# Modulation products of a two-block network: whole 1 MB pieces through the weights' ring instead of quarter pieces with a ring of their own

## The chip, the cores and the metric

The kernel runs on one core of a Trainium2 chip, alone. Every time is in microseconds (us) on the device. The kernel was timed in three runs: 2586.94, 2588.70 and 2591.15 us, median 2588.7. One further execution was recorded by the profiler; all rows below come from that one.

The engines are named as the profile names them: PE multiplies matrices (PEld is its loading of the stationary operand), DVE and ACT do elementwise work, POOL is a third, slower elementwise engine, and SP issues nearly all the transfers from DRAM. Each engine runs its instructions in the order in which they were written out at build time; SP does too, so that a transfer whose buffer is not free holds up all transfers behind it.

## The reference

A first block (norm, a mixer with recurrences and attention, output product, feed-forward) is followed by two layers of a second block. Each of these layers is steered by modulation vectors, which depend on nothing but the two vectors `c` and `c_ctx`:

```python
def ada_mods(cvec, w, b):                      # w [1024, 6144], b [6144]
    m = jax.nn.silu(cvec) @ w + b
    return jnp.split(m[:, None, :], 6, axis=-1)

def modulate(h, shift, scale):
    return h * (1.0 + scale) + shift

def first_block(x, ...):                       # one layer
    z = rms_norm(x, norm_mix[l]) @ w_in[l]
    ...                                        # four mixers of 256 columns each
    x = x + mixed @ w_out[l]
    gu = rms_norm(x, norm_ffn[l]) @ w_gate_up[l]
    return x + (silu(gu[..., :D_FF]) * gu[..., D_FF:]) @ w_down[l]

def second_block(x, c, ctx, c_ctx, ada_w, ada_b, ...):
    for l in range(2):
        sh1_l, sc1_l, ga1_l, sh2_l, sc2_l, ga2_l = ada_mods(c, ada_w[l], ada_b[l])
        sh1_c, sc1_c, ga1_c, sh2_c, sc2_c, ga2_c = ada_mods(c_ctx[None, :], ada_w[l], ada_b[l])
        hl = modulate(rmsnorm(xl, norm1_g[l]), sh1_l, sc1_l)
        ...                                    # mixer, expert feed-forward
```

Here `x` has 512 tokens of 1024 features and `ctx` 256 tokens. Everything is float32. The modulation products of a layer multiply 2 rows by a matrix of 24 MB, so that both layers read 48 MB for them.

## The kernel before

Products of activations and weights are done in three passes with a high and a low part of each operand. `wload` (line 190) brings a weight block of up to [128, 2048] float32 (1 MB) into a buffer of the tag `raw`, a ring of three (two in the projection of layer 0), and `split` makes `hi` on ACT (line 208) and `lo` on DVE (line 209) from it, each in a ring of two. The raw buffer is free once both have read it.

The modulation products run beside other work. `ada_setup` lists 192 pieces (layer, group g of 2048 columns, block k of 128 rows, quarter j of 512 columns). `fill(n)` (line 874) emits the next n of them at the place of the call. `ada_piece` (line 876) loads 128 x 512 float32 (256 KB) into a ring of its own, of four buffers in the first block and three in layer 0 (`ada_open`), and multiplies it with one matrix product (line 883): the stationary operand has 32 columns (two are used), and quarter j goes to column group j of the array (`tile_position=(0, 32 * j)`), so that four quarters fill the 128 rows of one PSUM bank. After eight k the bank gets its bias (line 892), is written to DRAM as rows (line 894) and turned into columns (line 898).

`fill` is called with 8 before each of the four token tiles of the attention's preparation in the first block (line 558), with 2 after each of its 32 attention units (line 686), with 5 before each projection of layer 0 (line 979), and at the end with what is left (line 936). The first 96 pieces belong to layer 0, the others to layer 1.

The order in which instructions stand on an engine is not that of the source: a scheduler writes it out at build time. It moves instructions past others where data and buffers allow.

The stages of the profile around the change are, by time in the recorded execution: preparation of the attention (141.5 to 204.6 us, with a tile of relative-position biases written to DRAM as `skewd` and read back as `skew`), the attention (to 345.5), the output product with `w_out` (`b1_out`, lines 758 to 789, to 410), the norm before the feed-forward (`norm_T`, line 230, to about 436) and the feed-forward (to 797), the norm of layer 0 (to 823), and the projections of layer 0 (`l0_proj`, `project` at line 977, to 1108). In the attention `s` are scores, `p` probabilities, `t` their transposes, `c` the small compressed scores, `o` the output.

Of the kernel before, what the change touches and what calls it, by code (L numbers as in the profile page):

```python
# [9 lines left out]
F32 = mybir.dt.float32  # L10
# [9 lines left out]
P = 128  # L20
# [3 lines left out]
# order of the recurrence: prep stages A-D of two steps, m pieces of attention, s scans; then o pieces of the  # L24
# attention's output, r output tiles
# [10 lines left out]
def host_consts():  # L36
    """Arrays that depend on shapes alone."""
# [10 lines left out]
    # rope: row = t // 64, col = t % 64, 8 frequencies each  # L48
# [4 lines left out]
    cs = np.zeros((S, 2, 2, 2, 8), np.float32)        # [t, cos/sin, half, x1/x2, 8]  # L53
# [5 lines left out]
    # rope on 64-wide heads: 16 frequencies each  # L59
# [9 lines left out]
    # recurrence: chunk masks, rows (b|k) or (k|b) by columns (a|r) or (r|a)  # L69
# [16 lines left out]
class Net:  # L86
    def __init__(self, tc, I, ctx):
        self.tc, self.nc, self.I, self.ctx = tc, tc.nc, I, ctx
        self.n = 0
        self.taken = 0            # banks outside the roles  # L90
# [26 lines left out]
    def banks(self, **roles):  # L117
        """divide PSUM anew: role=(banks of a tile, number of tiles).  Tiles of a role are handed out in program
        order, so work that should overlap has roles of its own."""
# [22 lines left out]
    def rowb(self, pool, src, n, name, parts=P, queue=None):  # L142
        """a row of DRAM on every partition"""
        t = pool.tile([P, n], F32, name=name)
        (queue or self.nc.sync).dma_start(t[:parts], bass.AP(tensor=src.tensor, offset=src.offset,
                                                             ap=[[0, parts], [1, n]]))
        return t

    def col(self, pool, src, n, name, m=P):
        """DRAM vector of n*m -> [m, n], feature i*m+p at [p, i]"""  # L150
# [4 lines left out]
    def rsqrt(self, src, mul, eps, n, name, parts=P):  # L155
        """1/sqrt(src*mul+eps) for [parts, n] (bit-trick seed, three Newton steps)"""
# [13 lines left out]
    def rsqrt_s(self, src, mul, n, name):  # L170
        """1/sqrt(src*mul+1e-6) for [P, n]: square root and reciprocal, then a Newton step"""
# [18 lines left out]
    def wload(self, src, nk, n, name, k0=0, c0=0, pitch=None, kp=P, queue=None, pool=None, after=None):  # L190
        """weights rows k0.. (nk tiles of kp rows), columns c0..c0+n of a DRAM matrix -> (hi, lo) [P, nk, n]"""
# [22 lines left out]
    def norm_T(self, x, nt, hi, lo, work, scales, shifts=None, eps=1e-6, name="nt", segs=None,  # L214
               inplace=False):
        """x [P, nt, D] token-major -> hi/lo [P, 8, nt*128]: (x*rstd)*scale(+shift), features on partitions.
        scales/shifts: list over segments of [P, 8] columns; segs: list of (start, stop) tokens."""
# [28 lines left out]
    def norm_tile_T(self, x, t, hi, lo, work, g):  # L246
        """token tile t, x [P, D], normalised in place -> its columns of hi/lo, times g"""
# [16 lines left out]
    def qk_T(self, pool, src, nh, nt, dst1, dst2, t0, work, tag, same=False, role="p1"):  # L264
        """src [P tok, nh, 64] (one token tile) -> stacked operands, features on partitions.
        q: dst1[:, h, tok] = [hi; lo].  k (same): dst1 = [hi; hi], dst2 = [lo; lo]."""
        self.qk_turn(self.qk_split(src, nh, work, tag, same), nh, dst1, dst2, t0, role)

    def qk_split(self, src, nh, work, tag, same, joint=False):
        """joint: hi and lo parts in one tile, of a tag that serves both kinds"""  # L270
# [28 lines left out]
    def softmax(self, s, n, pout, rs, work, gate=None):  # L299
        """s [P, n] in PSUM -> pout [P, n] = exp(s-max) * gate / sum"""  # L300
# [12 lines left out]
    def block1(self):  # L313
        """-> x [P, 6, D] (context rows, then the first block's output) and its pool"""
# [3 lines left out]
        ada.enter_context(self.ada_open(ada, 4))  # L318
# [19 lines left out]
    def b1_mix(self, y, es):  # L338
# [11 lines left out]
        with ExitStack() as e3:  # L350
# [7 lines left out]
            # token-major columns 1280..2703  # L358
# [14 lines left out]
            # features on partitions: 0..1279  # L373
# [40 lines left out]
    def b1_lru(self, u, y, tp):  # L414
# [10 lines left out]
        # sp = softplus(-lam) = max(-lam,0)+ln(1+exp(-|lam|))  # L425
# [3 lines left out]
        nc.vector.tensor_sub(sp[:, 1], sp[:, 1], sp[:, 0])   # min(lam,0)-max(-lam,0) = -|lam| + min.. fixed below  # L429
# [4 lines left out]
        # log_a = -8*sp*r, r=(1+tanh)/2 -> log_a = c4*tanh + c4, c4 = -4*sp  # L434
# [1985 lines left out]
```

## Time and profile before

| | |
|---|---|
| median of three timed runs | 2588.7 us |
| span of the recorded execution, first to last instruction | 2585.1 us |
| median less span | 3.6 us |
| PE busy over the span | 91% |
| DVE, ACT, POOL busy | 60%, 43%, 12% |
| mean granted PE clock | 0.934 of 2.4 GHz |

The page gives the span of the recorded execution and no total of it beside the span; what lies around the span is taken from the median, 3.6 us. The busy shares are means over stages with different limits; PE is the busiest engine, and stage by stage it is either busy throughout or waits for something that can be named. A matrix product in float32 appears as two records on PE (and two weight loads on PEld), so that 192 products of line 883 are 384 records.

### The profile page before, as it was taken

What the parts mean: (1) busy time and instruction counts of PE and PEld (TensorE: products, weight loads), DVE (VectorE), ACT (ScalarE), POOL (GpSimd) and SP (SyncE); (2) the same over time, 40 slices, a digit from 0 to 9 for tenths busy, and PEclk for the clock granted to TensorE, in tenths of its full rate; (3) what the DMA queues carried; (4) which work ended last, traced back from release to release, by engine and by line L of the source; (5) the groups of instructions that cost most, each with busy time, mean ns of one, the idle gap of its engine ahead of it and who ended that gap; (6) DMA issues with size and microseconds to landing.
All of it is one profiled execution on the core that took longest, in us unless ns stands there. A gap on an engine that the chain in (4) does not pass through costs nothing. (4 is left out here: it accounts for less than half of the span.)

```text
span 2585.1 us, 37766 instructions
## 1 busy us (share of the span) xinstructions
PE 2340.3 (91%) x14345; PEld 1811.0 (70%) x14345; DVE 1548.9 (60%) x2915; ACT 1108.8 (43%) x1836; POOL 320.3 (12%) x409
## 2 busy tenths in 40 slices
PE   8959998999998999979899998899995889998994
PEld 6825466888885666767678887697873777777773
DVE  4464544333324436366666656976886987755885
ACT  4443333222223323344445443334675466634773
POOL 0001201000000000001111112301012113301112
PEclk9989989999998999975899999889997999998997
DMA  5345445333214456373445435747997320045995
GB/s 178 98 162 160 145 150 193 129 110 112 93 56 137 167 172 193 123 179 87 104 105 118 110 72 152 230 154 260 339 357 265 111 66 1 1 148 201 376 360 194
DMA packets 388531, 411.58 MB, mean 159 GB/s; under 512 B 119780, under 2 KB 301476, under 8 KB 388348
## 3 DMA queue, kind: packets, MB, share of 16 engines
q1 hardware_dynamic: 377708, 370.84, 46.0%
q0 software_dynamic: 10640, 38.31, 4.0%
q8 instruction: 114, 1.87, 0.3%
q14 instruction: 69, 0.57, 0.1%
HBM read 340.46 MB, written 70.65 MB: 159 GB/s over the span
## 5 line engine op out<-in xcount | busy, mean ns | idle before, releaser
L883 PE MATMUL adaps<-adaw,silu_c 128*32 128x512 f32 x384 | 143.9, 636 | 37.9 <-DMA adaw<-in_ada_w_dram 37.2
L304 DVE TENSOR_REDUCE mx<-s 128x1 f32<-128x768 f32 (+4 forms) x160 | 121.4, 760 | 83.5 <-PE s L188 61.8
L209 DVE TENSOR_TENSOR eg_l<-eg_w,eg_h 128x2048 fp32r<-128x2048 f32 x66 | 150.8, 2287 | 19.3 <-ACT eg_h L208 19.0
L208 ACT ACTIVATE eg_h<-eg_w 128x2048 fp32r<-128x2048 f32 x66 | 126.5, 1919 | 28.1 <-DMA eg_w<-in_moe_w_up_dram 12.7
L186 PE MATMUL p<-lhh,abw_hi 128*128 128x512 f32 (+1 forms) x336 | 116.6, 347 | 0.0
L187 PE MATMUL p<-lhl,abw_hi 128*128 128x512 f32 (+1 forms) x336 | 115.8, 345 | 0.0
L188 PE MATMUL p<-lhh,abw_lo 128*128 128x512 f32 (+1 forms) x336 | 115.4, 343 | 0.0
L187 PE MATMUL g<-eg_l,xh 128*128 128x512 f32 x264 | 107.3, 406 | 5.5 <-DVE eg_l L209 5.2
L186 PE MATMUL g<-eg_h,xh 128*128 128x512 f32 x264 | 108.2, 410 | 3.5 <-ACT eg_h L208 3.4
L188 PE MATMUL g<-eg_h,xl 128*128 128x512 f32 x264 | 104.8, 397 | 0.0
L209 DVE TENSOR_TENSOR ed_l<-ed_w,ed_h 128x2048 fp32r<-128x2048 f32 x33 | 75.6, 2292 | 43.7 <-ACT ed_h L208 43.6
L995 POOL COPY ms<-mc 128x2 f32<-128x2 f32 x30 | 10.8, 359 | 651.4 <-ACT mc L990 636.5
L2026 POOL DMA_INDIRECT xe<-h2d,idx x33 | 45.4, 1376 | 312.1 <-PE x L2040 237.0
L186 PEld LDWEIGHTS p<-lhh,abw_hi 128*128 128x128 f32 (+1 forms) x336 | 62.3, 185 | 24.6 <-issue 11.3
L310 POOL TENSOR_SCALAR ap<-ap,rc 128x768 f32<-128x768 f32 x64 | 58.4, 912 | 155.2 <-DVE rc L307 92.9
L187 PEld LDWEIGHTS p<-lhl,abw_hi 128*128 128x128 f32 (+1 forms) x336 | 62.3, 185 | 15.6 <-issue 8.0
L310 POOL TENSOR_SCALAR mlp<-mlp,rc 128x768 f32<-128x768 f32 (+1 forms) x48 | 41.6, 866 | 248.5 <-DVE rc L307 198.2
L883 PEld LDWEIGHTS adaps<-adaw,silu_c 128*32 128x32 f32 x384 | 19.2, 110 | 75.7 <-DMA adaw<-in_ada_w_dram 55.5
L188 PEld LDWEIGHTS p<-lhh,abw_lo 128*128 128x128 f32 (+1 forms) x336 | 62.7, 187 | 12.0 <-issue 3.8
L186 PE MATMUL p<-h2h,wg_hi 128*128 128x512 f32 x176 | 68.8, 391 | 0.7 <-ACT h2h L234 0.7
L187 PE MATMUL p<-h2l,wg_hi 128*128 128x512 f32 x176 | 68.7, 390 | 0.0
L188 PE MATMUL p<-h2h,wg_lo 128*128 128x512 f32 x176 | 68.7, 390 | 0.0
(750 smaller groups left out, 6818.7 us busy)
## 6 DMA issues: line engine op xcount, KB each, us to landing
adaw<-in_ada_w_dram SPq DMA_DIRECT2D x192, 256.0 KB
eg_w<-in_moe_w_gate_dram SPq DMA_DIRECT2D x66, 512.0 KB
eg_w<-in_moe_w_up_dram SPq DMA_DIRECT2D x66, 512.0 KB
ed_w<-in_moe_w_down_dram SPq DMA_DIRECT2D x33, 1024.0 KB
yslot<-ye SPq DMA_DIRECT2D x33, 512.0 KB
wg_w<-in_w_gate_up_dram SPq DMA_DIRECT2D x11, 1024.0 KB
wu_w<-in_w_gate_up_dram SPq DMA_DIRECT2D x11, 1024.0 KB
wd_w<-in_w_down_dram SPq DMA_DIRECT2D x10, 1024.0 KB
```

The lines of the kernel that those rows point to most:

```text
L186: mm(out, lh, rh, start=start, stop=False)
L187: mm(out, lh, rl, start=False, stop=False)
L188: mm(out, ll, rh, start=False, stop=stop)
L208: self.nc.scalar.activation(hi, raw, AF.Copy)
L209: self.nc.vector.tensor_sub(lo, raw, hi.bitcast(F32))
L304: nc.vector.tensor_reduce(mx, s, axis=AX.X, op=OP.max, negate=True)
L310: nc.gpsimd.tensor_scalar(pout, pout, rc, 1.0, op0=OP.mult, op1=OP.mult)
L883: nc.tensor.matmul(self.ada_ps[32 * j:32 * j + 32], self.silu_c[:, k], w, start=k == 0, stop=k == 7, tile_position=(0, 32 * j), skip_group ...
L995: nc.gpsimd.tensor_copy(s[:, a:b:b - a - 1], c[:, a + 1:b - 1:b - a - 3])
L2026: nc.gpsimd.indirect_dma_start(out=x, out_offset=None, in_=h2, in_offset=bass.IndirectOffsetOnAxis(ap=idx, axis=0))
```

## The change

A piece is now a whole k block of a group: 128 x 2048 float32, 1 MB, loaded by one transfer into a buffer of the weights' ring (`raw`), and its four quarters are multiplied by four products written one after another. There are 48 pieces. `fill(n)` counts quarters as before and emits a piece for each four that are due. The ring of its own is gone; the weights' ring of layer 0's projections has three buffers instead of two. (The file with the change also has its comments removed, and its line numbers are one lower from line 882 on; line 882 there is line 883 here.)

```diff
-        ada.enter_context(self.ada_open(ada, 4))
+        ada.enter_context(self.ada_open(ada))
...
-        for l in range(2):
-            for g in range(3):
-                for k in range(8):
-                    for j in range(4):
-                        self.todo.append((l, g, k, j))
+        self.todo = [(l, g, k) for l in range(2) for g in range(3) for k in range(8)]
+        self.due = 0
...
     def fill(self, n):
-        for _ in range(min(n, len(self.todo))):
+        self.due += n
+        while self.due >= 4 and self.todo:
+            self.due -= 4
             self.ada_piece(*self.todo.pop(0))
...
-        if k == 0 and j == 0:
+        if k == 0:
             self.ada_ps = self.adaps.tile([P, 512], F32, tag="ada", bufs=1, name=f"adaps{l}{g}")
-        w = self.apool.tile([P, 512], F32, tag="adaw", bufs=self.adabufs, name="adaw")
-        c0 = g * 2048 + j * 512
-        nc.sync.dma_start(w, I["ada_w_2"][l, k * P:(k + 1) * P, c0:c0 + 512])
-        nc.tensor.matmul(self.ada_ps[32 * j:32 * j + 32], self.silu_c[:, k], w, start=k == 0, stop=k == 7,
-                         tile_position=(0, 32 * j), skip_group_check=True)
-        if k < 7 or j < 3:
+        w = self.wpool.tile([P, 2048], F32, tag="raw", bufs=self.raws, name="adaw")
+        nc.sync.dma_start(w, I["ada_w_2"][l, k * P:(k + 1) * P, g * 2048:(g + 1) * 2048])
+        for j in range(4):
+            nc.tensor.matmul(self.ada_ps[32 * j:32 * j + 32], self.silu_c[:, k], w[:, j * 512:(j + 1) * 512],
+                             start=k == 0, stop=k == 7, tile_position=(0, 32 * j), skip_group_check=True)
+        if k < 7:
             return
...
-        with ExitStack() as es, self.ada_open(es, 3):
+        with ExitStack() as es, self.ada_open(es):
             self.l0_proj(x, xpool)
-            self.fill(96)
+            self.fill(192)
...
-            self.open_weights("right", 2)
+            self.open_weights("right", 3)
```

The scheduler makes another order of it. On PE, in the middle of the attention, between a compressed unit and the scores of the next, stood before (adaps are the modulation products):

```order
L654 MATMUL c_2128<-ident,pc 31x128 x2
L883 MATMUL adaps_1748<-adaw,silu_c 32x512
L657 MATMUL o_2133<-pTc,kc_1608 64x128 x2
L883 MATMUL adaps_1748<-adaw,silu_c 32x512
L642 MATMUL c_2142<-kcT_1636,qT 128x32
L643 MATMUL c_2142<-kcT_1641,qT 128x32
L617 MATMUL t_2170<-ident,p 128x128
L617 MATMUL t_2174<-ident,p 128x128
L883 MATMUL adaps_1748<-adaw,silu_c 32x512
L597 MATMUL s_2186<-k_1146,qT 128x256
```

At such a place of the changed kernel stands, on the same engine:

```order
L654 MATMUL c_2170<-ident,pc 31x128 x2
L882 MATMUL adaps_1740<-adaw,silu_c 32x512 x4
L657 MATMUL o_2061<-pTc,kc_1560 64x128 x2
L642 MATMUL c_2183<-kcT_1588,qT 128x32
L643 MATMUL c_2183<-kcT_1593,qT 128x32
L617 MATMUL t_2211<-ident,p 128x128 x2
L617 MATMUL t_2216<-ident,p 128x128 x2
L642 MATMUL c_2197<-kcT_1588,qT 128x32
L643 MATMUL c_2197<-kcT_1593,qT 128x32
L597 MATMUL s_2225<-k_1146,qT 128x384
```

Three single products at three places have become four in a row at one. Not every piece stays whole: the scheduler also writes rows of one and of three. Over the program the modulation products stand in 118 rows before and in 59 now. Counting up to four in a row as one run, and stage by stage, they make 54 runs and now 25 from the first score to the end of the attention, 13 and now 11 ahead of that, 7 and now none from the output product to the end of the feed-forward, 8 and now 4 in the norm of layer 0, and 38 and now 28 in its projections.

On SP, the queue of the transfers, from the weights of the transposed products (`winT`) on, stood before (`wout` are the four loads of the output product):

```order
L201 DMA winT_w<-in_w_in_dram 128x8x256 x5
L201 DMA wout_w<-in_w_out_dram 128x2x1024 x4
L397 DMA rb<-in_rel_bias_dram 32x4
L399 DMA oh<-in_c_bucket_dram 32x992
L145 DMA past<-in_c_past_dram 4x992
L882 DMA adaw<-in_ada_w_dram 128x512 x4
```

In the changed kernel the same stretch reads:

```order
L201 DMA winT_w<-in_w_in_dram 128x8x256 x5
L880 DMA adaw<-in_ada_w_dram 128x2048 x3
L397 DMA rb<-in_rel_bias_dram 32x4
L399 DMA oh<-in_c_bucket_dram 32x992
L145 DMA past<-in_c_past_dram 4x992
L880 DMA adaw<-in_ada_w_dram 128x2048
```

The loads of `wout` have moved behind the last piece of layer 0, to the end of the attention, where the queue now reads:

```order
L880 DMA adaw<-in_ada_w_dram 128x2048 x3
L889 DMA adar<-in_ada_b_dram 32x512
L327 DMA x<-in_x_dram 128x1024 x2
L201 DMA wout_w<-in_w_out_dram 128x2x1024 x2
L893 DMA modrow_83<-adar 2x512 x4
L152 DMA onorm<-in_out_norm_dram 128x8x1
L201 DMA wout_w<-in_w_out_dram 128x2x1024 x2
L201 DMA wg_w<-in_w_gate_up_dram 128x8x256
```

Pieces and weights take the three raw buffers in turn, so each transfer of either kind waits until the tile three places ahead of it has been read.

## Rows read from the trace of the kernel before

**Rows 1.** The page, busy time and share of each engine.

```profile
PE 2340.3 (91%) x14345; PEld 1811.0 (70%) x14345; DVE 1548.9 (60%) x2915; ACT 1108.8 (43%) x1836; POOL 320.3 (12%) x409
```

**Rows 2.** Stages: length; busy PE, PEld, DVE, ACT, POOL (records); clock; DMA share; GB/s.

```profile
179.00:204.60 25.60, 22.35 (x110) 11.21 (x110) 14.40 (x49) 17.41 (x40) 0.19 (x1) 0.93 0.65 214
204.60:345.50 140.90, 138.98 (x778) 69.37 (x777) 72.54 (x307) 49.88 (x177) 30.61 (x64) 0.98 0.50 147
345.50:410.00 64.50, 61.27 (x269) 48.93 (x268) 33.90 (x42) 16.51 (x21) 0.00 (x0) 0.87 0.46 151
410.00:470.00 60.00, 53.03 (x231) 37.61 (x230) 22.74 (x34) 21.59 (x27) 12.52 (x22) 0.97 0.65 224
823.00:1108.00 285.00, 280.71 (x1460) 202.61 (x1461) 132.63 (x262) 88.57 (x124) 11.98 (x31) 0.99 0.51 158
```

**Rows 3.** The same view of the modulation products alone, on PE.

```profile
179.00:204.60 25.60, 10.41 (x30) 0.93 0.65 214
204.60:345.50 140.90, 59.18 (x139) 0.98 0.50 147
345.50:410.00 64.50, 3.15 (x10) 0.87 0.46 151
410.00:470.00 60.00, 7.78 (x18) 0.97 0.65 224
470.00:797.00 327.00, 2.12 (x12) 0.99 0.29 95
823.00:1108.00 285.00, 41.22 (x132) 0.99 0.51 158
```

**Rows 4.** Timeline of PE: start, length, instruction, records, idle before and its releaser.

```profile
142.09 1.06 PE L883 MATMUL adaps<-adaw,silu_c 128*32 128x512 f32 x8
...
186.28 1.04 PE L883 MATMUL adaps<-adaw,silu_c 128*32 128x512 f32 x2
187.26 0.88 PE L294 MATMUL p<-ident,qh 128*128 128x128 f32 x6
```

**Rows 5.** Waits of PE from 200 to 345: total us, times, longest.

```profile
PE s L597 <- ACT p L305: 1.4, 3, 0.6
PE t L617 <- POOL p L310: 0.4, 1, 0.4
```

**Rows 6.** Timeline of PE in the preparation, and where the attention ends.

```profile
174.53 1.92 PE L883 MATMUL adaps<-adaw,silu_c 128*32 128x512 f32 x2 [20.83 <-DMA adaw<-in_ada_w_dram]
...
346.77 11.03 PE L764 MATMUL p<-ones,ysq 128*128 128x1 f32 x64 [0.63 <-ACT ysq L761]
...
361.47 0.79 PE L188 MATMUL p<-wout_hi,yl 128*128 128x512 f32 x1 [2.61 <-DVE yl L775]
```

**Rows 7.** Timeline of DVE in the preparation.

```profile
143.47 2.29 DVE L209 TENSOR_TENSOR wout_lo<-wout_w,wout_hi 128x2048 fp32r<-128x2048 f32 x1 [4.54 <-ACT wout_hi L208]
...
173.77 0.20 DVE L551 TENSOR_SCALAR hgain<-hgain 128x64 f32<-128x64 f32 x1 [11.65 <-DMA hgain<-in_fox_qk_norm_dram]
```

**Rows 8.** Timeline of ACT before the attention, and at its end.

```profile
141.52 1.91 ACT L208 ACTIVATE wout_hi<-wout_w 128x2048 fp32r<-128x2048 f32 x1 [4.77 <-PE p L187]
...
346.09 1.14 ACT L761 ACTIVATE ysq<-y 128x512 f32<-128x512 f32 x2
```

**Rows 9.** Waits of PE from 410 to 470, 797 to 823, 823 to 1108, in this order.

```profile
PE adaps L883 <- DMA adaw<-in_ada_w_dram: 6.2, 3, 2.7
...
PE adaps L883 <- DMA adaw<-in_ada_w_dram: 6.2, 3, 2.9
...
PE adaps L883 <- DMA adaw<-in_ada_w_dram: 2.6, 4, 0.7
```

**Rows 10.** Timeline at layer 0's start: first load of its weights, first use.

```profile
792.33 2.09 SPq L201 DMA_DIRECT2D abw_w<-in_ab_w_in_dram  x2
...
799.12 1.91 ACT L208 ACTIVATE abw_hi<-abw_w 128x2048 fp32r<-128x2048 f32 x1 [5.57 <-DMA abw_w<-in_ab_w_in_dram]
801.07 2.29 DVE L209 TENSOR_TENSOR abw_lo<-abw_w,abw_hi 128x2048 fp32r<-128x2048 f32 x1 [1.00 <-ACT abw_hi L208]
```

**Rows 11.** Transfers of layer 0's weights from 785 to 1108: durations of issue, min/median/max in ns.

```profile
L201 SPq DMA_DIRECT2D abw_w<-in_ab_w_in_dram x12: 378/390/1438, 792.3 to 1039.8; - x12
```

More of the change, by code (lines that the diff above doesn't have):

```diff
@@ L849, in ada_setup, with ada_open @@
         self.modrow = [self.dram.tile([2, 6144], F32, name=f"modrow{l}") for l in range(2)]
-        self.todo = []
-        for l in range(2):
-            for g in range(3):
-                for k in range(8):
-                    for j in range(4):
-                        self.todo.append((l, g, k, j))
+        self.todo = [(l, g, k) for l in range(2) for g in range(3) for k in range(8)]
+        self.due = 0
     @contextmanager
-    def ada_open(self, es, bufs):
-        self.adabufs = bufs
+    def ada_open(self, es):
         self.apool = es.enter_context(self.pool("ada", 1))
@@ L871, in fill, with ada_piece @@
     def fill(self, n):
-        for _ in range(min(n, len(self.todo))):
+        self.due += n
+        while self.due >= 4 and self.todo:
+            self.due -= 4
             self.ada_piece(*self.todo.pop(0))
-    def ada_piece(self, l, g, k, j):
+    def ada_piece(self, l, g, k):
         nc, I = self.nc, self.I
-        if k == 0 and j == 0:
+        if k == 0:
             self.ada_ps = self.adaps.tile([P, 512], F32, tag="ada", bufs=1, name=f"adaps{l}{g}")
-        w = self.apool.tile([P, 512], F32, tag="adaw", bufs=self.adabufs, name="adaw")
-        c0 = g * 2048 + j * 512
-        nc.sync.dma_start(w, I["ada_w_2"][l, k * P:(k + 1) * P, c0:c0 + 512])
-        nc.tensor.matmul(self.ada_ps[32 * j:32 * j + 32], self.silu_c[:, k], w, start=k == 0, stop=k == 7,
-                         tile_position=(0, 32 * j), skip_group_check=True)
-        if k < 7 or j < 3:
+        w = self.wpool.tile([P, 2048], F32, tag="raw", bufs=self.raws, name="adaw")
[4 more added lines that the diff above has]
+        if k < 7:
             return
```

## The prediction

> **What bounds the kernel now.** I read the shares of the engines first: PE is busy 91% of the span, DVE 60%, ACT 43%, POOL 12% [rows 1]. Then the stages, where the shares differ. In the attention PE works 138.98 of 140.90 us at a clock of 0.98, while DVE has 72.54, ACT 49.88 and POOL 30.61 [rows 2]. In layer 0's projections it works 280.71 of 285.00 [rows 2]. Both are bound by PE, so a us taken off PE there is a us of the program as long as nothing else comes late. In the attention hardly anything is late now: PE waits three times for ACT (1.4 us) and once for POOL (0.4) [rows 5]. In the preparation PE has 22.35 of 25.60, but ACT has 17.41 and DVE 14.40 there and the three form a chain [rows 2]; the norm before the feed-forward is 88% busy on PE (53.03 of 60.00) and waits 6.2 us for pieces [rows 2, 9].
>
> Third, the modulation products alone: 59.18 us of PE in the attention, 10.41 in the preparation, 41.22 in the projections, 3.15, 7.78 and 2.12 in the stretches between [rows 3]. What four of them cost together is already in the trace: by luck of the order four stand in a row at 142.09 (eight records), and take 1.06 us; one alone (two records) takes 1.04, and the next instruction begins 0.98 after it [rows 4]. So the four column groups run beside each other, and a run of up to four costs what one costs. What counts is the number of runs, not of products.
>
> At that point the Trainium skill has a figure that speaks against me: "TensorE: Matmul & The Clock Gate", in the section on the measured speedup of packed tiles, gives 2.38 times for three column tiles, not three. By it a run of three costs 1.26 times a single product; the row shows 1.06 against 1.04 for four, and the measurement decides.
>
> **The change part by part.** Times are of the profiled execution: span 2585.1 us, and 3.6 around it to the median of 2588.7. I subtract from the median.
>
> *Attention.* The order has 54 runs before and 25 after. Everything else PE does there is 138.98 − 59.18 = 79.80 us. With 25 × 1.05 = 26.3 for the runs and the 1.9 of idle time kept, the stage takes 108.0 in place of 140.9: −32.9. Against it: 29 places at which a product filled a gap are gone, and at each a unit's softmax may now show. How long such a gap is the trace does not show, because it is filled. Below it is nothing; above the longest wait for ACT that is seen, 0.6 us, at all 29 places: 17.4. At the mean of the three seen, 1.4 / 3 = 0.47, it would be 13.6. DVE, at 72.54, still has 35 us of room in 108, so it doesn't bound as a whole. I take 8, somewhat over half of that, since only some of the places will show a gap. **−25** (−33 to −15).
>
> *Start and preparation.* Of the eleven runs now ahead of the attention five stand behind the first transposes of q; there were ten. That is 10.41 − 5 × 1.05 = 5.2 less on PE, half of which I count, because DVE and ACT hold the chain there. The stall of 20.83 us at 153.70 is put down to a piece's load, but DVE waits 11.65 us for `hgain` to land until 173.77, and the transposes of q come 2.6 us behind the piece [rows 6, 7]: the landing in the queue behind the big `skewd` tile is the cause, and it stays. Twelve products now stand before the first transposes where four and eight stood, and one of the 1 MB pieces sits in the queue between the bias and `skewd`. Four times the bytes of a piece delay that chain by something that no row prices; I take between nothing and 4. **−2** (−6 to +4).
>
> *Output product to feed-forward.* No run is left here, and seven stood before. The 3.15 from 345.50 on go whole, since PE is 61.27 of 64.50 busy [rows 2, 3]: −3. In the norm 7.78 of products and 6.2 of waits go [rows 3, 9], 14 together, but PE was filling time in which it would have waited for DVE and ACT (22.74 and 21.59): without them it has 45.25 of 60 to do. I take 5. In the feed-forward 2.12: −2. **−10** (−12, or −17 if the norm gives all, to −6).
>
> *The loads of `wout` come late.* They stood before the attention; the splits of the first of them on ACT at 141.52 (1.91) and DVE at 143.47 (2.29) sat in waiting time [rows 7, 8]. Now all four are issued at the attention's end, and two of ACT's splits stand there before its last copies. What covers them: from the squares of y at 346.09 through the row sums (11.03 on PE) to the first product with `wout` at 361.47 are 15.4 us [rows 6, 8]. A weight's load took 6.8 us from its issue at 792.33 to the start of its split, and its split 1.91 + 2.29, so it is ready after 11.0 [rows 10]. The first fits in that cover; what doesn't are the two splits ahead of work that the chain needs, 2 × 1.91 = 3.8 on ACT. If the cover is gone, it is the 11.0 of one load. **+4** (0 to +10).
>
> *Norm of layer 0.* PE waits 6.2 us in it for pieces [rows 9], and its products fall from eight runs to four. But three 1 MB pieces share the queue with the first weights of layer 0. **−4** (−8 to +3).
>
> *Projections.* 28 runs stand where 38 stood: 28 × 1.05 = 29.4 in place of 41.22, −11.8; the waits for pieces (2.6) [rows 3, 9] may go with them. Pieces and weights share three buffers now, so I give 3 back. **−11** (−15 to −2).
>
> The sum is −25 − 2 − 10 + 4 − 4 − 11 = −48: 2588.7 − 48 = **2541**. The rest of the program, layer 1 with its mixer and both expert stages, has no modulation products and keeps its time.
>
> **The rivals.**
>
> *The attention is bound by its own chain.* The products filled waiting time, and without them PE waits for softmax. For it: each unit goes PE, DVE, ACT, POOL, PE in turn, and scores have three buffers. Against it: only 1.8 us of waits there [rows 5], and no engine over 52% busy beside PE. The stage would shrink by some 10 in place of 25: 2556.
>
> *PE's clock falls.* An engine with gaps may be granted less. For it: 0.87 from 345.50 to 410.00, where PE multiplies single columns [rows 2, 6]; against it: 0.97 from 410.00 to 470.00 with PE 88% busy [rows 2]. At a mean of 0.80 over the 106 us of PE's work left in attention and preparation it would cost 106 × (0.98 / 0.80 − 1) = 24: 2565.
>
> *Runs cost more than one product.* If a tenth of each further product in a run of four showed, 3 × 0.1 × 1.05 = 0.3, the runs left in preparation, attention, norm and projections (5 + 25 + 4 + 28 = 62) would cost 62 × 0.3 = 19 more: 2560. The row of four in a row speaks against it [rows 4]. The page of the Trainium skill named above would make it 0.27 a run and 2558.
>
> *Slower: weights come late in the projections.* SP issues twelve loads of layer 0's weights between 792.3 and 1039.8 [rows 11], and each now takes its turn in three buffers behind 1 MB pieces. A piece's buffer is free only when PE has come to its products, and these stand among the products of the block before; the load, and with it all transfers behind it on SP, starts only then. Ready after 11.0 us [rows 10], it would be exposed by half of this where the products left cover the rest: 12 × 5.5 = 66, and with −48 + 66 the time is 2607. It decides from (48 + 5) / 12 = 4.4 us per load. For it: even the small pieces are awaited for 2.6 us there [rows 9]. Against it: PE has 239.5 us of other work there (280.71 − 41.22), 20 per load, and a third buffer.
>
> *The change doesn't merge what it says.* The scheduler could pull a piece's products apart again. The order shows that it does for some (runs of one and three), and these are counted; a null result is left for what else may undo the gain.
>
> **How the numbers follow.** Forecast 0.68; attention bound by its chain 0.14; clock 0.07; dearer runs 0.03; weights late 0.06; no change 0.02. The ends of the parts, each at its best, add to −79, and at their worst to −6; as they are not all at one end together, the forecast's own range is 2520 to 2560. The stated range, 2516 to 2576, takes in the first three rivals, and leaves out the slower one and the tail. What a measurement of this kernel can tell from no change is 0.2%, 5.2 us: faster by more than that 0.89 (the first cases, less a few hundredths for their tails), within it 0.05, slower 0.06.
>
> **What would show it.** In the profile after, attention should last about 116 us from its first score, with the modulation products at about 26 us of PE and a run of three or four at 1.05; waits of PE for ACT or POOL there of some 8 us. If that stage lasts 130 with waits of 25, the chain bounds it. A granted clock under 0.9 there shows the second rival. From the attention's end to the first product with `wout` about 19 to 20 us should pass instead of 16.0 (345.50 to 361.47). In the projections PE should wait for no `abw` load longer than a few us; if the waits for `abw_hi` or `abw_lo` add to over 50, the slower rival holds. The stall before the transposes of q should stay near 20 us. The prediction is wrong in its core if four products in a row take 2 us or more, or if the products' busy time in the attention stays near 59.

## The result

| | before | changed |
|---|---|---|
| median of four timed runs (lowest to highest) | 2589.9 us (2586.9 to 2596.1) | 2534.9 us (2529.5 to 2539.8) |
| span of the profiled execution | 2585.1 us | 2527.8 us |

The ratio is 0.9778, with a 95% interval of 0.9759 to 0.9798: 55.0 us less, where 48 were forecast. It lies inside the forecast's own range. The spans differ by 57.3 us, and the stages account for it. First the stages' beginnings, in the timeline of PE of the changed kernel (start, length, instruction; idle time before it and its releaser in brackets):

```profile
200.88 0.31 PE L597 MATMUL s<-k,qT 128*128 128x128 f32 x1
...
314.68 0.49 PE L764 MATMUL p<-ones,ysq 128*128 128x1 f32 x3 [1.21 <-ACT ysq L761]
...
326.83 0.77 PE L186 MATMUL p<-wout_hi,yh 128*128 128x512 f32 x1
...
386.71 0.80 PE L186 MATMUL p<-h2h,wg_hi 128*128 128x512 f32 x1 [0.56 <-ACT h2h L234]
...
757.97 0.45 PE L230 MATMUL p<-ident,x 128*128 128x128 f32 x1 [6.36 <-DVE x L225]
...
781.57 0.50 PE L186 MATMUL p<-lhh,abw_hi 128*128 128x512 f32 x1 [0.76 <-ACT l0n1tmp L241]
...
1091.10 0.58 PE L186 MATMUL s<-mlak,mlaq 96*128 96x256 f32 x1
```

The same places of the kernel before that no row above shows:

```profile
204.61 0.33 PE L597 MATMUL s<-k,qT 128*128 128x128 f32 x1
...
357.66 0.77 PE L186 MATMUL p<-wout_hi,yh 128*128 128x512 f32 x1
...
423.48 0.50 PE L186 MATMUL p<-h2h,wg_hi 128*128 128x512 f32 x1 [0.67 <-ACT h2h L234]
...
796.90 0.66 PE L230 MATMUL p<-ident,x 128*128 128x128 f32 x2 [5.37 <-DVE x L225]
...
822.92 0.50 PE L186 MATMUL p<-lhh,abw_hi 128*128 128x512 f32 x1
...
1150.85 0.58 PE L186 MATMUL s<-mlak,mlaq 96*128 96x256 f32 x1
```

| stage, from PE's rows | before | changed | difference | forecast |
|---|---|---|---|---|
| start to the first scores | 204.6 | 200.9 | −3.7 | −2 |
| attention, to the row sums | 142.2 | 113.8 | −28.4 | −25 |
| row sums to the feed-forward | 76.7 | 72.0 | −4.7 | −4 |
| feed-forward | 373.4 | 371.3 | −2.1 | −2 |
| norm of layer 0 | 26.0 | 23.6 | −2.4 | −4 |
| projections, to layer 0's second scores | 327.9 | 309.5 | −18.4 | −11 |
| the rest | 1434.3 | 1436.7 | +2.4 | 0 |

(In the third and fourth rows the forecast's −10 and +4 are put to the places that they were worked out for.)

The page's line of busy times shows where this comes from: PE lost 62.9 us of work [rows 1], the other engines next to none.

```profile
PE 2277.4 (90%) x14345; PEld 1808.3 (72%) x14345; DVE 1545.7 (61%) x2915; ACT 1109.3 (44%) x1836; POOL 321.7 (13%) x409
```

By stretches of the changed kernel (length; busy PE, PEld, DVE, ACT, POOL; clock; DMA share; GB/s), preparation, attention, the norm of layer 0 and the projections:

```profile
179.00:200.90 21.90, 18.37 (x121) 11.15 (x121) 14.88 (x53) 16.68 (x40) 0.19 (x1) 0.90 0.64 231
200.90:314.00 113.10, 110.16 (x755) 66.82 (x752) 70.65 (x307) 54.45 (x180) 30.54 (x64) 0.97 0.57 188
...
758.00:781.60 23.60, 14.82 (x73) 7.24 (x73) 16.55 (x30) 13.73 (x23) 0.00 (x0) 0.74 0.80 277
781.60:1091.30 309.70, 291.67 (x1642) 223.95 (x1643) 158.06 (x321) 106.23 (x158) 13.95 (x45) 0.97 0.59 183
```

The same view of the modulation products of the changed kernel alone (PE, PEld), which answers to [rows 3]; none stand from the row sums to the end of the feed-forward:

```profile
179.00:200.90 21.90, 5.68 (x32) 0.81 (x32) 0.90 0.64 231
200.90:314.00 113.10, 26.93 (x118) 3.71 (x118) 0.97 0.57 188
...
758.00:781.60 23.60, 6.22 (x24) 0.90 (x24) 0.74 0.80 277
781.60:1091.30 309.70, 28.82 (x168) 4.59 (x168) 0.97 0.59 183
```

In the attention 59.18 us have become 26.93, where 25 runs at 1.05 were worked out as 26.3. PE is still busy 97% of the stage, in a stage that is a fifth shorter. At the stall before the transposes of q the timelines of PE, DVE and ACT read now:

```profile
141.89 2.78 PE L882 MATMUL adaps<-adaw,silu_c 128*32 128x512 f32 x24
...
176.43 1.92 PE L882 MATMUL adaps<-adaw,silu_c 128*32 128x512 f32 x2 [22.02 <-DMA adaw<-in_ada_w_dram]
179.10 1.12 PE L294 MATMUL p<-ident,qh 128*128 128x128 f32 x4 [0.76 <-DVE qh L280]
...
173.81 0.20 DVE L551 TENSOR_SCALAR hgain<-hgain 128x64 f32<-128x64 f32 x1 [12.08 <-DMA hgain<-in_fox_qk_norm_dram]
...
173.70 0.68 ACT L518 ACTIVATE f<-p,fb 4x512 f32<-4x512 f32 x1 [18.35 <-DMA fb<-in_fox_f_bias_dram]
```

Twelve products in three runs take 2.78 us there. The product of the piece that PE waits for starts 2 us later than before (176.43 against 174.53 [rows 6]; the piece is four times as large), but the first transposes begin at 179.10 against 179.02: DVE, which waits for `hgain`, sets the time, now as before [rows 7].

### The profile page after: what moved, and what is told of

Its sections match the earlier page's. It is cut to its first block, busy times and chain, and to the rows that moved or that the text cites. A ratio compares the mean times of both kernels' runs of the same rounds, so it can differ in the third digit from the quotient of the medians.

```text
span 2527.8 us, 37507 instructions
## 1 busy us (share of the span) xinstructions
PE 2277.4 (90%) x14345; PEld 1808.3 (72%) x14345; DVE 1545.7 (61%) x2915; ACT 1109.3 (44%) x1836; POOL 321.7 (13%) x409
## 5 line engine op out<-in xcount | busy, mean ns | idle before, releaser
L208 ACT ACTIVATE eg_h<-eg_w 128x2048 fp32r<-128x2048 f32 x66 | 126.5, 1918 | 28.7 <-DMA eg_w<-in_moe_w_up_dram 12.2
L186 PE MATMUL p<-lhh,abw_hi 128*128 128x512 f32 (+1 forms) x336 | 115.3, 343 | 0.8 <-ACT l0n1tmp L241 0.8
L882 PE MATMUL adaps<-adaw,silu_c 128*32 128x512 f32 x384 | 75.3, 640 | 29.6 <-DMA adaw<-in_ada_w_dram 29.6
L186 PE MATMUL p<-wd_hi,ah 128*128 128x512 f32 x176 | 68.5, 389 | 0.2 <-DVE x L836 0.2
L186 PE MATMUL p<-h2h,wu_hi 128*128 128x512 f32 x176 | 68.7, 390 | 0.0
```

The source lines that it names most:

```text
L186: mm(out, lh, rh, start=start, stop=False)
L208: self.nc.scalar.activation(hi, raw, AF.Copy)
L882: nc.tensor.matmul(self.ada_ps[32 * j:32 * j + 32], self.silu_c[:, k], w[:, j * 512:(j + 1) * 512], start=k == 0, stop=k == 7, tile_positi ...
```

## The experiments

Two theories stood at first. By the first, what pays is the number of runs of modulation products on PE, at 1.05 us for a run of up to four, and PE bounds the stages. By the rivals it is the writing of four products together (A), the large transfers (B), or fewer changes between kinds of work (D); and by C the attention's own chain of engines soon takes over as the bound. Times below are medians of four to six runs (two for the kernel without products in the attention), and ratios are to the kernel before on the same chip.

**Merging in the source alone**, in the kernel before:

```diff
     def fill(self, n):
-        for _ in range(min(n, len(self.todo))):
-            self.ada_piece(*self.todo.pop(0))
+        self.due += n
+        while self.due >= 4 and self.todo:
+            self.due -= 4
+            for _ in range(4):
+                self.ada_piece(*self.todo.pop(0))
...
-        with ExitStack() as es, self.ada_open(es, 3):
+        with ExitStack() as es, self.ada_open(es, 4):
```

> The kernel before, with quarters emitted four at a time in the source, but still loaded as 256 KB pieces through a ring of their own of four (in layer 0 too). In the order that comes out the modulation products stand in 108 runs of up to four (before 120, changed kernel 68), 52 of them in the attention (54, 25). Theory (a run of up to four costs what one costs, 1.05 us, and PE bounds): 12 runs fewer than before, of which 10 in the projections: 2590 - 12 = 2578, attention from first scores to the squares of y 139 us (before 141.5, changed 113.1). Rival A (it is the writing of four products together in the source that pays): 2540 and an attention of 115. Rival B (large transfers pay): near 2590.

Measured: 2577.3 us, ratio 0.9944 (0.9923 to 0.9964) to the kernel before, where 2578 was expected; beside it the kernel before took 2593.1, so that it is 15.9 us less and not 12. The modulation products' work in the projections and in the attention (timeline stretches of this kernel, products alone):

```profile
820.60:1137.70 317.10, 31.60 (x123) 4.32 (x122) 0.95 0.53 161
204.80:345.90 141.10, 58.43 (x139) 7.70 (x138) 0.96 0.50 150
```

In the attention little changed: the scheduler tears four products that were written together into 52 runs. That it does so because each waits for its own 256 KB is argued, and fits the next run. In the projections, where it found 28 runs, 10.8 us went (327.9 to 317.1); the ring of the pieces also has four buffers there in place of three, and what these are worth was not separated. Rival A is out.

**The large load alone**, in the changed kernel (`fill` emits single quarters again):

```diff
-        for j in range(4):
-            nc.tensor.matmul(...)              # four products of the piece (l, g, k)
+        if j == 0:
+            self.ada_w = self.wpool.tile([P, 2048], F32, tag="raw", ...)
+            nc.sync.dma_start(self.ada_w, ...)
+        nc.tensor.matmul(...)                  # one product, of the quarter (l, g, k, j)
```

> The changed kernel, with 1 MB loads through the weights' ring, but the four products of a piece emitted one at a time, as before. The order has 81 runs (68 in the changed kernel), 33 in the attention (25), 31 in the projections (28), 6 in the norm (4). Theory (runs): 13 x 1.05 = 14 above the changed kernel, 2549; attention 121 us. Rival A (products must be written together): near 2585, attention over 135. Rival B (the large load alone pays, however the products stand): 2535, attention 113.

Measured: 2548.6 us, ratio 0.9834 (0.9796 to 0.9871), where 2549 was expected from 81 runs; the attention took 123.2. So the load of 1 MB through the shared ring brings most of the merging by itself: four products become ready at once, and the scheduler places them together though they were written apart. Rival B is right about the cause in the source and wrong about the mechanism, since the time follows the runs: against the changed kernel the attention is 9.4 us longer for 8 runs more and the projections 4.3 for 3. That the totals differ by 13.7 for 13 runs is in part luck, because the rest of the program, which has no products, differs by 9.8 between the two traces. Pieces of 1 MB in a ring of their own were not tried.

**All four products on one column group**:

```diff
-            nc.tensor.matmul(self.ada_ps[32 * j:32 * j + 32], ..., tile_position=(0, 32 * j), ...)
+            o = 32 * j if k == 7 else 0
+            nc.tensor.matmul(self.ada_ps[o:o + 32], ..., tile_position=(0, o), ...)
```

> The changed kernel, with the four products of a piece on the same column group of the array instead of four (only the last piece of each group of eight keeps its four column groups). This changes what is computed: the quarters of seven pieces of eight are summed into one. Theory (four column groups run beside each other, so a run costs one product): now each product costs its own 1 us, so four in a row take about 4.1 us instead of 1.06, the modulation products' busy time on PE rises from 67.6 to some 170, and the time from 2535 by 60 to 100, to about 2615 (2595 to 2640). Rival D (what pays is fewer changes between kinds of work on PE, not the parallel groups): four in a row stay near 1 to 1.5 us, and the time is 2535 plus 27 more runs x 1.05 = 2563 at most.

Measured: 2728.2 us. In the timeline of PE, products on one group, and then four on four groups (the last of eight pieces) in the same kernel:

```profile
147.39 13.92 PE L883 MATMUL adaps<-adaw,silu_c 128*32 128x512 f32 x32
...
197.40 1.90 PE L883 MATMUL adaps<-adaw,silu_c 128*32 128x512 f32 x4
...
199.60 1.07 PE L883 MATMUL adaps<-adaw,silu_c 128*32 128x512 f32 x8
```

On one group each further product costs 0.86 us (two take 1.90); on four groups four take 1.07. The products' busy time is 170.5 us, as expected, and rival D is out. The total went beyond the expectation of 2595 to 2640, and for another reason: up to the experts of layer 0 the kernel is 62 us behind the changed one, within the expectation, and the other 129 us come in the experts. Other modulation vectors send the tokens to other experts: this kernel makes 36 loads `ed_w` of experts' weights, the changed one 33. From the experts on PE works 760.7 us in place of 707.3, and it waits for the tokens of three overflow tiles, which the changed kernel does not have:

```profile
PE x L2041 <- DMA xe<-h2d,ovi: 33.5, 3, 13.1
```

These two make 87 of the 129; the other 42 are idle time that was not followed up.

What this says of the Trainium skill's figure ("TensorE: Matmul & The Clock Gate", the section on the measured speedup), 2.38 times for three column tiles: here four tiles side by side take 1.07 us, and one after the other 0.98 + 3 × 0.86 = 3.56, which is 3.3 times for four. That is 0.83 of the number of tiles, and the figure is 0.79 of it, so set against products that follow one another the two nearly agree. The prediction set the figure against a product that stands alone and made a dearer run of it. For that the trace has 1.07 against 1.04, so a run of four is no dearer here.

**Runs kept whole**, tried first with a section that the scheduler may not take apart (`with self.tc.tile_critical():` around the four products):

> The changed kernel with the four products of a piece kept together by the scheduler: 48 runs of four (68 before this edit), 15 in the attention (25), 21 in the projections (28), 9 ahead of the attention (11). Theory (runs, PE bounds): 20 x 1.05 = 21 less, 2514, attention 113.1 - 10.5 = 102.6. Rival C (the attention is bound by its own chain of engines once the products are few): attention stays over 108, and the total falls by 10 or less, 2525 to 2535.

Measured: 2637.9 us, ratio 1.0194 (1.0164 to 1.0225), slower than before. The waits of PE in this kernel show why (total us, times, longest):

```profile
PE adaps L883 <- DMA hgain<-in_fox_qk_norm_dram: 18.9, 1, 18.9
...
PE adaps L883 <- ACT hsq L541: 7.9, 2, 6.5
PE adaps L883 <- DMA cw<-in_nsa_cmp_w_dram: 7.1, 2, 5.2
```

The products wait for tiles that they don't read: the section brings waits of its own. This edit says nothing of runs. The same aim without such a section, by an edge of issue order and a priority:

```diff
-        for j in range(4):
-            nc.tensor.matmul(...)
+        first = mm(0)
+        with self.tc.high_priority(offset=1000), self.tc.issue_after(first.ins):
+            for j in range(1, 4):
+                mm(j)
```

> The changed kernel with the second to fourth product of a piece placed directly behind the first by the scheduler's own priorities, with no section around them that brings waits of its own: 48 runs of four (changed kernel 68), 14 in the attention (25), 21 in the projections (28), 10 ahead of the attention (11). Theory (a run costs 1.05 us, PE bounds): 20 x 1.05 = 21 less than the changed kernel, 2514; from the first scores to the row sums 113.8 - 11.6 = 102. Rival C (the attention is bound by its own chain of engines once the products are few): that stage stays over 109, total 2521 to 2530.

Measured: 2523.6 us, ratio to the kernel before 0.9751 (0.9733 to 0.9770). The attention fell to 100.9 us, where 102 were expected, and the projections to 302.9; seven runs fewer would make 309.5 − 7.4 = 302.1. Its attention, all engines:

```profile
203.20:304.00 100.80, 95.43 (x749) 63.06 (x747) 70.61 (x307) 53.26 (x181) 30.74 (x64) 1.00 0.62 211
```

The total is 10 above the expected 2514, given back in small pieces: 2.3 us later first scores, 4.9 us more from the row sums to the feed-forward, and 4.3 between layer 0's second scores and the experts, where no code differs. This version beats the kernel before. Because the step from the changed kernel is small, both were timed again on one chip:

> The changed kernel once more, beside the two below on one chip, since these are compared with it. 2535 (2530 to 2540); from the first product of layer 0's projections to the first scores of its second mixer half 309 to 312 us.

> The kernel with whole runs of four once more. Theory: 9 to 13 us below the changed kernel on the same chip, with the attention at 100 to 102 us from the first scores to the row sums (113 to 114 in the changed kernel). Rival (the two differ by scatter only): within 4 us of it.

Measured: 2537.1 us (2530.2 to 2548.0) and 2526.1 (2515.5 to 2532.1), ratios 0.9788 (0.9757 to 0.9820) and 0.9747 (0.9719 to 0.9774). The 11 us are there again; the intervals of the ratios overlap, but five of the six runs are below every one of the changed kernel's. The whole runs' attention was 106.6 this time and not 100 to 102, at a clock of 0.94 in place of 1.00; the changed kernel's was 115.3.

**No products in the attention:**

```diff
             next(f, None)
-            self.fill(2)
...
             self.b1_ffn(x, pool, es)
+            self.fill(64)
```

> The changed kernel with no modulation products in the attention; the 16 pieces due there are written after the feed-forward instead. Looked at for the attention alone. Theory (PE bounds the attention, the other engines have room): from the first scores to the row sums 113.8 - 26.9 = 87, at most 90. Rival C (its own chain bounds it): 95 or more, with waits of PE for ACT, DVE or POOL of over 8 us. The prediction's term of 8 us given back as new waits would be seen here as about 95.

Measured: 103.3 us in the attention (2554.3 in all). PE's waits for POOL, ACT and DVE add to 11.2 us, so the waits that rival C named are there at this end. The two longest, and then stretches of 20 us (columns as before):

```profile
PE t L618 <- POOL p L310: 3.8, 4, 2.3
PE s L598 <- ACT p L305: 3.3, 5, 1.5
```

```profile
198.70:220.00 21.30, 16.56 (x75) 13.47 (x73) 11.76 (x33) 7.86 (x20) 4.26 (x5) 0.68 0.65 164
220.00:240.00 20.00, 19.30 (x123) 14.98 (x123) 12.24 (x56) 8.83 (x33) 4.68 (x8) 0.83 0.39 126
```

Two things hold it up. PE is idle for 103.2 − 90.55 = 12.7 us over the stage, and in the first 41 us the clock is 0.68 and 0.83, which by these rows costs some 16.56 × 0.32 + 19.30 × 0.17 = 8.6. But a lower clock early in the attention is no mark of this kernel. Here are the second 20 us of the changed kernel, and the first 20 us of the two traces of whole runs, which are the same program:

```profile
220.90:240.90 20.00, 19.79 (x113) 12.87 (x112) 10.26 (x42) 7.78 (x29) 3.66 (x7) 0.83 0.37 125
...
203.20:223.20 20.00, 17.74 (x137) 13.89 (x135) 13.45 (x59) 8.27 (x29) 5.00 (x9) 1.00 0.77 208
...
200.50:220.50 20.00, 17.86 (x95) 14.22 (x93) 10.81 (x43) 7.17 (x26) 3.56 (x7) 0.70 0.63 144
```

So the stages have to be compared without what the clock takes. The table estimates it in the same way for each trace, as PE's busy time in the first 40 us times the missing share of the clock (later in the stage the clock is 1.00):

| kernel | runs in the attention | first scores to row sums | PE idle in it | clock, estimate | without it |
|---|---|---|---|---|---|
| before | 54 | 142.2 | 2.5 | 3.3 | 138.9 |
| merged in the source | 52 | 141.1 | 3.6 | 5.0 | 136.1 |
| large load alone | 33 | 123.2 | 3.6 | 4.8 | 118.4 |
| changed | 25 | 113.8 | 3.6 | 3.4 | 110.4 |
| changed, second trace | 25 | 115.3 | 3.6 | 4.8 | 110.5 |
| kept whole | 14 | 100.9 | 5.5 | 0.0 | 100.9 |
| kept whole, second trace | 14 | 106.6 | 5.4 | 6.2 | 100.4 |
| none | 0 | 103.3 | 12.7 | 8.6 | 94.7 |

The two traces of a kernel, 1.5 and 5.7 us apart, agree within 0.5 without the clock. From 54 to 25 runs the stage loses 28.5 / 29 = 0.98 us a run, nearly the whole price of one; from 25 to 14 it loses 9.5 / 11 = 0.86, and from 14 to none 6.2 / 14 = 0.44. The attention's own chain shows gradually, most of it below 14 runs. So the waits keep the stage from the theory's 87 us, and without the clock it is just under rival C's 95. That it is longer than the 100.9 of whole runs is the clock's doing.

**Two raw buffers in layer 0** (`self.open_weights("right", 2)`), twice:

> The changed kernel with two raw buffers in layer 0 instead of three, so that pieces and weights of the projections share two. Runs are the same in number (68). Theory (the third buffer is not what pays; two hold up loads now and then): 0 to 10 us above the changed kernel, 2535 to 2545, all of it in the projections. Rival F (without the third buffer the weights come late behind the pieces): 15 us or more above it, with waits of PE for abw_hi or abw_lo.

> The changed kernel with two raw buffers in layer 0 once more. Theory (the third buffer is worth 6 us in the projections, the term that the prediction had with the other sign): 4 to 9 us above the changed kernel on the same chip, the stretch at 314 to 317 us. Rival (the 5.7 us between the two first traces were scatter): within 3 us of it, the stretch at 308 to 312.

Measured: 2544.6 us, and on the same chip as the repeated changed kernel (2537.1) 2542.1, so 5 us more there, with overlapping intervals (0.9814, 0.9786 to 0.9842, against 0.9788). In the traces the stretch from the first projection to layer 0's second scores took 315.2 and 316.0 us, with three buffers 309.5 both times: 6 us, which repeat. In both the norm ahead is longer too (26.7 and 29.0 against 23.6 and 24.3), so that layer 0's second scores come 8 us later than in the changed kernel's two traces. All engines in the stretch, with two buffers:

```profile
784.20:1099.50 315.30, 291.86 (x1645) 224.47 (x1642) 156.98 (x319) 105.71 (x156) 15.27 (x45) 0.96 0.60 187
```

PE's work is the same as with three (291.86 against 291.67); its idle time is 23.4 us against 18.0. No single wait stands out.

**The stall before the transposes of q**: the loads of `fb` and `hgain` written ahead of the bias tile's round through DRAM, together with whole runs.

```diff
+        nc.sync.dma_start(fb, ...)
+        nc.sync.dma_start(gn[:, 0:2]..., ...)
+        nc.sync.dma_start(gn[:, 2:6]..., ...)
         with ExitStack() as e3:
             self.b1_bias(skew, ...)
```

> The same kernel (runs kept whole), and in addition the small loads fb and hgain are written ahead of the bias tile's round through DRAM (skewd) instead of behind it. Theory on the stall before the transposes of q (the small loads land behind skewd, and DVE's 12.1 us for hgain is the chain): the preparation is 12 us shorter, first scores at about 189 instead of 201, total 2514 - 12 = 2502. Rival E (the stall is the wait of PE for the modulation piece's own load, as the profile's releaser says): first scores stay at 199 to 201, total 2514.

Measured: 2538.6 us, ratio 0.9817 (0.9794 to 0.9841), slower than whole runs alone. The first scores came at 181.1 in place of 203.2, 22 us earlier where 12 were expected, and the timeline of PE shows the transposes at 164.0 in place of 180.0 (179.1 in the changed kernel). The second row is the first product of the compressed keys, at 210.3 with whole runs alone:

```profile
163.99 1.99 PE L294 MATMUL p<-ident,qh 128*128 128x128 f32 x8 [10.59 <-DVE qh L280]
...
219.24 7.04 PE L720 MATMUL c<-crh,cw 128*128 128x32 f32 x32 [3.85 <-DVE crh L705]
```

So the small loads held DVE, as the theory has it, and the first scores did not stay where rival E put them. But the order changed with the edit: the piece for which PE waited 21.8 us ahead of the transposes with whole runs alone now has its products behind the first scores. With that piece still ahead PE could not have come to the transposes before it landed at 177, so this run does not part the two waits. In the changed kernel SP issues the load that reads `skewd` back, for which it must have landed, at 173.45, and DVE goes on with `hgain` at 173.81. That small loads waited behind the 2 MB of `skewd` fits what the Trainium skill says in "DMA: Bandwidth & Descriptors", on queues, rings and completion order: each DMA engine takes the descriptors of a ring in their order. But the attention took 138.0 us, all that was won and more. PE came to the first modulation products of the attention only 30 us after the first scores (at 211.1), and the store of the modulation rows, which waits for them, stands on SP ahead of the loads for the compressed keys. The wait of SP in that stretch, and two of this kernel's stretches of 20 us:

```profile
SPq L899 <- DVE adar L897: 29.8, 1, 29.8
```

```profile
200.00:220.00 20.00, 13.94 (x105) 8.50 (x103) 6.67 (x20) 5.01 (x14) 2.57 (x4) 0.92 0.12 7
220.00:240.00 20.00, 16.65 (x76) 14.13 (x75) 4.96 (x30) 2.14 (x8) 0.20 (x1) 0.50 0.77 259
```

For 20 us almost nothing is loaded (7 GB/s), PE has gaps, and its clock falls to 0.50 for the next 20. PE is idle for 18.1 us of the stage, in place of 5.5. Then also `gb` and the two `cpos` loads were written early:

> The kernel with runs kept whole and fb and hgain loaded early, and now also gb and the two cpos loads early. In e11 the first scores came 22 us earlier than with whole runs alone, but the attention lasted 138.0 in place of 100.9. Theory G (SP stood 29.8 us at a store of modulation rows, whose pieces came late, and the cpos loads stood behind it, so the compressed keys came late, PE had gaps and its clock fell to 0.5): with cpos ahead, the attention lasts 100 to 112, total 2524 - 22 + up to 11 = 2502 to 2514. Rival H (the second load of the compression's weights stands behind the same store, and the late pieces fill no gaps): the attention stays over 125, total 2525 or more.

Measured: 2532.4 us, ratio 0.9785 (0.9762 to 0.9809), with an attention of 129.8, as rival H has it: these loads gave back 8 of the 37 us. SP waits at the same store:

```profile
SPq L904 <- DVE adar L902: 28.5, 1, 28.5
```

Which of the things that still stand behind the store holds the attention up was not separated, and how the 20 us of the preparation could be freed without this jam was not tried.

## Why the prediction was right

*The mechanism and its price held.* That four column groups run beside each other [rows 4], and that runs are what costs, was read from one row of the trace before; the kernel with one group shows it, with 1.90 us for two products on one group and 1.07 for four on four. 26.93 us of products in the attention against 26.3 worked out, and the stages of the two half changes, bear it out; that their totals fall within 1 us of what was expected is closer than such totals scatter.

*What is given back in the attention.* The prediction took 8 us; it was 4.5 (28.4 less in place of 32.9), and mostly not what the term stood for. Of gaps in which softmax shows there is little: by the rows PE's idle time is 2.9 in place of 1.9, and its waits for ACT, DVE and POOL up to the row sums add to 3.5. PE's other work is 83.2 us in place of 79.8. The clock does not explain that, since it costs 3.3 us before and 3.4 after by the estimate above. A run was priced at 1.05, but the next instruction begins 0.98 after it [rows 4], and 29 runs at 0.98 are 28.4: part of what looks given back was in the price. So the rival with its own chain as the bound was wrong at 25 runs; it shows in part below 14.

*The projections were mis-sized: −11 forecast, −18.4 measured.* It is the step that was furthest off. The merging was sized rightly: the products' work fell from 41.22 [rows 3] to 28.82 us, −12.4 where −11.8 was worked out. But the shared ring was entered with 3 us given back. With two raw buffers that holds: PE is idle 23.4 us in the stretch, against 20.3 before. The third buffer, which the change brings too and which got no term, makes it 18.0. It is worth 6 us in this stretch, with the same number of runs in the program. The slower rival had the same place with the sign reversed. Of waits for these weights the view lists 1.6 us for `abw_lo` and none for `abw_hi`. PE's other work fell by 3.4 us as well (266.3 to 262.9), which no term forecast; its cause stays open. The stretch of the kernel before, all engines:

```profile
822.90:1150.85 327.95, 307.62 (x1606) 225.20 (x1605) 157.46 (x319) 104.95 (x156) 15.77 (x45) 0.97 0.53 161
```

*The late loads of `wout`* were put at +4 and are covered. The two splits on ACT end before the squares of y begin, as its timeline shows, and PE waits for no `wout`. From the first row sum to the first product with `wout` pass 12.2 us in place of 10.9. The prediction took the product at 361.47 for the first; that is one with `yl`, and the first stands at 357.66, so the cover was 11.6 us and not 15.4. Behind it a wait of 2.6 for `yl` has gone [rows 6].

```profile
307.49 1.91 ACT L208 ACTIVATE wout_hi<-wout_w 128x2048 fp32r<-128x2048 f32 x1
...
311.41 1.90 ACT L208 ACTIVATE wout_hi<-wout_w 128x2048 fp32r<-128x2048 f32 x1
...
314.01 1.14 ACT L761 ACTIVATE ysq<-y 128x512 f32<-128x512 f32 x2
```

*The two norms.* From the row sums to the feed-forward −4.7 against −4 is luck, since two misses cancel: up to the first product with `wout` it is +1.3 in place of +4, and from there −5.9 in place of −8. That less than the 14 us of the norm came is as the prediction had it: in place of the pieces PE now waits for DVE. In layer 0 the gain was 2.4 of 4, because the waits for pieces were exchanged rather than removed. The waits of PE in these two stretches, in the order of the program:

```profile
PE p L230 <- DVE n2xn L225: 8.3, 1, 8.3
...
PE p L230 <- DVE x L225: 6.4, 1, 6.4
PE p L230 <- ACT l0n1tmp L241: 5.4, 2, 4.3
PE adaps L882 <- DMA adaw<-in_ada_w_dram: 2.6, 1, 2.6
```

*The clock* did not fall on the whole (0.97 against 0.98 in the attention). That it can was no idle rival: it fell to 0.50 for 20 us where the products came late, and between two traces of whole runs it makes 6 us of the attention by the estimate above.

*The rest* should have kept its time and is 2.4 us longer. The part from layer 0's second scores to the experts (the first product with `eg_h`) took between 620 and 630 us in all these kernels, whose code does not differ there, so this is scatter.

## What to carry to other kernels

Small matrix products that use a quarter of the array cost as much alone as four on four column groups (1.04 and 1.06 to 1.07 us here), so count runs, not products, and read the price of a run from a place where the order happens to make one. What stands together in the order is decided by what becomes ready together: one load for four products did more than four products written in a row. Taking filler work out pays its price until the stage's own chain shows; here 0.98 us a run down to 25 runs, and less than half of that for the last 14. Before two traces are compared stage by stage, what the granted clock took in each has to be set aside: it can be as large as the difference that is looked for.

## What was not expected

Two traces of the same program had a granted clock of 1.00 and 0.70 in the first 20 us of the attention. Without any products there it was 0.68 and 0.83 in the first 41 us; that the filler work would have held it up is not shown. It fell to 0.50 where PE had been 70% busy for 20 us before. A transfer that waits for a result (the rows of modulation, 28.5 and 29.8 us) stopped all loading on its queue, and made a preparation 22 us shorter into a total 15 us longer. An indivisible section around four products cost 114 us over the same four products kept together by order and priority (2637.9 against 2523.6).
